# Two more FFN chunks as seven block products, two filler slots a cycle, and convolution taps issued one slot after their copy

## The chip, the cores and the metric

The kernel runs on one core of one Trainium2 chip. The metric is the device time of one launch in microseconds; lower is better. An engine is called by its short name: PE (TensorE, matmuls; PEld are its weight loads), DVE (VectorE), ACT (ScalarE), POOL (GpSimd) and SP (SyncE, which issues most DMAs).

## What is computed

A trunk of two layers over x of 512 tokens by 1024 features, all in float32. Layer 0 mixes tokens by dilated window attention, layer 1 by a gated linear recurrence (RG-LRU). Behind each mixer stands a gated convolution FFN, which is the part that matters here:

```python
def causal_dwconv(x, w, b):
    K = w.shape[0]
    S = x.shape[1]
    xp = jnp.pad(x, ((0, 0), (K - 1, 0), (0, 0)))
    out = b
    for k in range(K):
        out = out + xp[:, k:k + S] * w[k]
    return out

def conv_ffn(x, w_up, conv_w, conv_b, w_down):
    u = causal_dwconv(x @ w_up, conv_w, conv_b)
    g, v = u[..., :D_FF], u[..., D_FF:]
    return (jax.nn.gelu(g, approximate=True) * v) @ w_down
```

D_FF is 3072, the convolution has 3 taps, and each sublayer sits between two RMS norms and is added to x.

## The kernel before

**Precision.** Every float32 product is done as three float32r products: each operand is split into a high part (ACT rounds it, line 150) and a low part (DVE subtracts, line 151), and PE multiplies high by high, high by low and low by high. One *split* is thus one ACT instruction and one DVE instruction behind it. The split parts of weights live in 16 pairs of buffers (`whi`, `wlo`); `pump` splits the next piece in a fixed list after each tile or slot (in the seven stage one piece a slot), as far as buffers allow.

**The FFN.** The 3072 features of each half of `u` (the gate half g and the value half v) are worked in 12 *chunks* of 256. A half chunk is two tiles of 128 features by 512 tokens. Some chunks are made directly: a tile is 8 x 3 matmuls that are 512 wide. The chunks in `SEVEN` (3 to 10) go another way, a *chain* for each half chunk: the weights (1024 x 256) and the normed input (1024 x 512) are cut into 2 x 2 blocks, and seven block products of 12 matmuls, 256 wide, take the place of eight (Winograd's form of Strassen's method). It needs

- sums of weight blocks: two by DMA that adds into the raw weights (line 187, issued by POOL), two on DVE (lines 211 and 215, `across` and `lower`);
- sums of input blocks, made once per FFN by `token_sums` on DVE and split into the tiles `T` (four pairs; ACT casts them and DVE makes the low part);
- sums of products: ACT copies three products aside (`part`, line 1028); DVE adds one of them to the upper half when step 3 is done (line 1032, called the *join* here) and carries step 7's product over to the other half of its bank before step 4 writes the first half again (line 1037, the *carry*).

Then the convolution: ACT's *copy* `u` of the finished bank, with weight and bias (line 774), two DVE *taps* (line 776) that add the shifted bank to u, and, behind a gate half, ACT's gelu (line 789), behind a value half DVE's gate product (line 793).

**The order.** The schedule is written out by hand: each engine's instructions stand in the order in which the program emits them. In `seven` that order is a table of slots: chain n starts at slot `CYCLE * n`, and `AT` places its steps 1, 5, 2, 6, 3, 7, 4 at slots 0, 1, 2, 4, 5, 8 and 13 (13 being slot 3 of the next cycle). The slots in `FREE` (6, 7, 9) take *fillers*: quarters of the last two direct tiles, and *row products*, the first half of the down projection's columns for one block of 128 features and two of the four token tiles (6 matmuls, 512 wide), accumulated in four PSUM banks. Each block of features costs two splits, one of its row weights and one of its activation. A slot with nothing in it is not emitted. `later(n, f)` emits f after the PE work of the n+1st emitted slot from there on, ahead of that slot's pump: the join, the carry, the copy and the gelu or gate are emitted so.

```python
    AT = {1: 0, 5: 1, 2: 2, 6: 4, 3: 5, 7: 8, 4: 13}
    CYCLE, FREE = 10, (6, 7, 9)
```

Before the seven stage the FFN makes chunks 0 and 1 and, directly too, chunk 11 and half of chunk 2 (the other half of 2 is the fillers' quarters). `token_sums` starts with the first tile of chunk 1 and goes on by one step a tile. Behind the stage, `down` does the remaining row products.

Of the kernel before, what the change touches and what calls it, by code (L numbers as in the profile page):

```python
# [19 lines left out]
S = 512  # L20
# [15 lines left out]
TOE_BUFS = 2  # L36
CP_PAD = 8
WARM = 5
SEVEN = range(3, 11)
LAST, TAIL, REST = 11, 16, range(18, 22)  # L40
EARLIER = (0, 1, 2, 3, 22, 23, *range(4, 18))
AT = {1: 0, 5: 1, 2: 2, 6: 4, 3: 5, 7: 8, 4: 13}
CYCLE, FREE = 10, (6, 7, 9)
EARLY = 16
QUAD = {1: 0, 5: 2, 2: 3, 6: 4, 3: 6, 7: 8, 4: 12}
APART, ROUND = 7, 44
# [38 lines left out]
def kernel(  # L85
# [107 lines left out]
    def free_slots(n):  # L193

        end = CYCLE * n
        free = [CYCLE * c + r for c in range(n) for r in FREE][2:] + [end, end + 1]
        assert not {CYCLE * c + a for c in range(n) for a in AT.values()} & set(free)
        return free

    def stream(i0, n):  # L200

        items = []
        for c in range(n):
            i, o = i0 + c, CYCLE * c

            def left(i=i):
                add_rows(blocks(i)["w11"], plan[i][3][0][0][:, 0:4, P:256])

            def across(i=i):
                x = blocks(i)  # L210
                nc.vector.tensor_tensor(x["s1"], x["w11"], x["a22"], op=ALU.add)
# [17 lines left out]
        at = 8  # L229
# [128 lines left out]
    def side(steps, delay=1):  # L358
        sides.append([delay, steps])
# [405 lines left out]
    def ffn(layer, hT, post, pre):  # L765
        ca, cc = ffn_cols[layer]
        neg = cp.tile([P, 144], F32, tag="neg", name=nm("neg"))
        nc.vector.tensor_scalar(neg[:, 0:96], ca, -1.0, None, op0=ALU.mult)
        nc.vector.tensor_scalar(neg[:, 96:144], cc[:, 0:48], -1.0, None, op0=ALU.mult)

        def conv(ps, j, minus=False):
            u = gen(s="u")
            near, far, own = (neg, neg, neg[:, 96:144]) if minus else (ca, ca, cc)
            nc.scalar.activation(u, ps, AF.Identity, scale=own[:, j : j + 1], bias=cc[:, 48 + j : 49 + j])  # L774
            for d, wc in ((1, near[:, 48 + j : 49 + j]), (2, far[:, j : j + 1])):
                nc.vector.scalar_tensor_tensor(  # L776
                    u[:, d:], ps[:, : S - d], wc, u[:, d:], op0=ALU.mult, op1=ALU.add
                )
            return u

        gv, ready = {}, set()

        def begin(b, ps, j, minus=False):
            m = b % 2
            k = 2 * j + m
            u = conv(ps, 24 * (b // 2) + k, minus)
            if b < 2:
                gv[k] = u
                return lambda: nc.scalar.activation(u, u, AF.Gelu_apprx_tanh)
# [12 lines left out]
        def gen_load(*srcs):  # L802
            o = []

            def load():
                for src in srcs:
                    o.append(gen(s="dw"))
                    nc.sync.dma_start(o[-1].rearrange("p (k c) -> p k c", c=src.shape[-1]), src)

            return o, load  # L810

        def act(k):
            assert k in ready, k
            return gv[k]

        direct = []
        for k in EARLIER:
            w = ffn_w_down[layer][k * P : (k + 1) * P, 0:512].rearrange("(k p) c -> p k c", p=P)
            o, load = gen_load(w)
            direct.append((("rows", k), load, lambda o=o: [o[0]], 0))  # L820
            direct.append((("act", k), None, lambda k=k: [act(k)], 2))
        up["direct"] = direct
        T = []
        for j in range(SEVEN[0] - 1):
            if j:
                side(token_sums(hT, T), 0)
                tiles(j, chunk(), (0, 1))
                tiles(j, chunk(), (2, 3))
            else:
                feat_tiles(2, hT, lambda b, ps: begin(b, ps, j)(), True)  # L830
        for j in (SEVEN[0] - 1, LAST):
            tiles(j, chunk(), (0, 1))
        tiles(LAST, chunk(), (2, 3))
        prep, run = down(act, post, pre)
        return run(seven(hT, T, begin, chunk(), lambda: prep(2)))

    def down(act, post, pre):

# [75 lines left out]
    def token_sums(hT, T, first=False):  # L914

        if not first:
            assert len(sides) == 1
# [122 lines left out]

        return lambda n: lambda: step(n)

    def seven(hT, T, begin, last, prep):

        right = rights(hT, T)
        i0, acc, ends_at = state["next"], {}, CYCLE * 2 * len(SEVEN)

        def finish(b, ps, j, minus=False):
            later(1, begin(b, ps, j, minus))

        def ends(j, half):
            return lambda ps: finish(2 * half, ps, j), lambda ps: finish(2 * half + 1, ps, j, True)
# [7 lines left out]
            if pair[-1] == 3:  # L1060
                done(2)

        fill = []
        for m in range(2):
            fill += quarters(last, m, hT, lambda ps, m=m: finish(2 + m, ps, SEVEN[0] - 1))
        fill += [lambda k=k, p=p: rows(k, p) for k in EARLIER for p in ((0, 1), (2, 3))]
        steps = {}
        n = 0
        for j in SEVEN:
# [544 lines left out]
    for layer in range(2):  # L1614
        if layer:
# [8 lines left out]
        chunks = [(j, half) for j in range(SEVEN[0]) for half in range(2)]  # L1624
        chunks[-1:] = [(LAST, 0), (LAST, 1), chunks[-1]]
        for j, half in chunks + [(j, half) for j in SEVEN for half in range(2)]:
# [89 lines left out]
```

## Time and profile before

| what | value |
|---|---|
| median of 3 runs (lowest, highest) | 1420.18 us (1419.66, 1420.43) |
| the profiled execution: its own time | 1419.78 us |
| its span in the profile | 1418.0 us |
| granted PE clock, mean | 0.999 |
| seven stage of the first FFN, first step to last | 568 to 794 us |
| seven stage of the second FFN | 1108 to 1335 us |
| DMA, mean over the span | 141 GB/s |

A profile row of a timeline gives the start in us, the duration in us, the engine, the line, the operation and the tiles (out<-in), and in brackets the engine's idle time before it and what ended that idle time. A row of a group gives the count, then busy us and mean ns of one, then the idle time of the engine just before such instructions. Durations contain the time that an instruction overlaps the next one; starts of neighbours give the time for which it holds its engine. A row of the chain of waits gives start, length and what work ended last there.

### The profile page before, as it was taken

The page shows a single profiled execution, that of the slowest core. Times are in us where ns is not written, and L with a number is a line of the kernel's source. Part 1 is how long each engine was busy: PE and PEld are TensorE (multiplying, and loading weights), DVE is VectorE, ACT ScalarE, POOL GpSimd, SP SyncE. Part 2 cuts the span into 40 slices and gives each one's busy share as a digit, 9 for nine tenths or more (in the row PEclk, how much of TensorE's full clock was granted, in tenths as well). Part 3 has the DMA queues.
Part 4 walks back from the last instruction along what each step waited for, and adds up shares of the span by engine and source line. Part 5 has one row for each costly group of instructions (what it writes and reads, how often), then busy time and mean ns, then how long its engine had stood idle before and what let it go on. Part 6 is the DMA issues. An engine that isn't in the chain of part 4 may idle for free.

```text
span 1418.0 us, 23252 instructions
## 1 busy us (share of the span) xinstructions
PE 1407.8 (99%) x8597; PEld 1262.2 (89%) x8597; DVE 1108.9 (78%) x2173; ACT 782.5 (55%) x1622; POOL 215.3 (15%) x336
## 2 busy tenths in 40 slices
PE   9999999999999999999999999999999999999998
PEld 7888999999998898999999889888898999999886
DVE  6676898887866988988888758769788988888843
ACT  7343565353636554666656545589454655666641
POOL 0341332131310100212120001000101211111000
PEclk9999999999999999999999999999999999999999
DMA  7653464655665453756563632432444566665411
GB/s 227 180 144 111 120 181 152 173 160 164 172 189 187 153 178 82 171 120 164 120 156 84 221 119 90 134 119 73 136 149 112 120 139 144 154 130 127 167 57 59
DMA packets 167657, 199.79 MB, mean 141 GB/s; under 512 B 10432, under 2 KB 136856, under 8 KB 167288
## 3 DMA queue, kind: packets, MB, share of 16 engines
q1 hardware_dynamic: 123064, 153.34, 33.8%
q0 software_dynamic: 43632, 43.92, 16.6%
q8 instruction: 67, 1.10, 0.3%
q10 hardware_dynamic: 848, 1.05, 0.2%
q14 instruction: 46, 0.38, 0.1%
HBM read 179.31 MB, written 18.96 MB: 140 GB/s over the span
## 4 chain that ended last, share of the span: by engine, by line
PE 77%; DVE 4%; ACT 4%; issue 1%; DVEq 0%; ACTq 0%
PE ps L1019 31%; PE acc L413 25%; PE ps L413 13%; PE v L1212 6%; DVE wlo L151 1%; DVE xb L1517 1%; PE O L1424 1%; PE S L1358 1%; ACT whi L150 1%; ACT sig L1538 1%; PE tr L503 1%; ACT sig L1557 0%; ACT a L1555 0%; ACT xhi L150 0%; ACT th L1556 0%
## 5 line engine op out<-in xcount | busy, mean ns | idle before, releaser
L151 DVE TENSOR_TENSOR wlo<-raw,whi 128x512 fp32r<-128x512 f32 x608 | 397.2, 685 | 103.6 <-ACT whi L150 101.0
L150 ACT ACTIVATE whi<-raw 128x512 fp32r<-128x512 f32 x608 | 358.8, 625 | 156.4 <-PE ps L1019 53.1
L413 PE MATMUL ps<-hT,whi 128*128 128x512 f32 (+1 forms) x1216 | 327.5, 357 | 0.0
L1019 PE MATMUL ps<-T,whi 128*128 128x256 f32 x1536 | 280.4, 282 | 1.4 <-DVE ps L1037 1.4
L1019 PEld LDWEIGHTS ps<-T,whi 128*128 128x128 f32 x1536 | 238.9, 189 | 5.6 <-DVE ps L1037 2.0
L413 PEld LDWEIGHTS ps<-hT,whi 128*128 128x128 f32 x1216 | 214.8, 189 | 31.4
L413 PE MATMUL ps<-hT,wlo 128*128 128x512 f32 (+1 forms) x608 | 216.2, 356 | 0.0
L1019 PE MATMUL ps<-T,wlo 128*128 128x256 f32 x768 | 215.0, 280 | 0.0
L1019 PE MATMUL ps<-hT,whi 128*128 128x256 f32 x1152 | 212.8, 283 | 0.0
L1019 PEld LDWEIGHTS ps<-hT,whi 128*128 128x128 f32 x1152 | 181.5, 191 | 3.2
L1019 PE MATMUL ps<-hT,wlo 128*128 128x256 f32 x576 | 162.9, 283 | 0.0
L187 POOL DMA_DIRECT2D raw<-in_ffn_w_up_dram x64 | 82.5, 1320 | 433.8 <-DVE wlo L151 356.2
L1019 PEld LDWEIGHTS ps<-T,wlo 128*128 128x128 f32 x768 | 146.0, 190 | 0.0
L413 PE MATMUL acc<-whi,ahi 128*128 128x512 f32 x352 | 137.5, 391 | 0.0
L413 PE MATMUL acc<-whi,alo 128*128 128x512 f32 x352 | 137.2, 390 | 0.2
L413 PE MATMUL acc<-wlo,ahi 128*128 128x512 f32 x352 | 137.0, 389 | 0.0
L776 DVE SCALAR_TENSOR_TENSOR u<-ps,cols,u 128x511 f32<-128x511 f32 (+1 forms) x128 | 95.8, 749 | 45.7 <-ACT u L774 43.3
L413 PEld LDWEIGHTS ps<-hT,wlo 128*128 128x128 f32 x608 | 114.9, 189 | 16.5
L774 ACT ACTIVATE u<-ps,cols 128x512 f32<-128x512 f32 x64 | 49.8, 778 | 113.6 <-DVE ps L1032 69.9
L1019 PEld LDWEIGHTS ps<-hT,wlo 128*128 128x128 f32 x576 | 110.2, 191 | 0.0
L1212 PE MATMUL v<-whi,hT 128*128 128x512 f32 x320 | 106.5, 396 | 0.0
L1028 ACT ACTIVATE part<-ps 128x256 f32<-128x256 f32 x144 | 54.3, 377 | 70.8 <-PE ps L1019 67.3
(206 smaller groups left out, 2125.4 us busy)
## 6 DMA issues: line engine op xcount, KB each, us to landing
raw<-in_ffn_w_up_dram SPq DMA_DIRECT2D x48, 1024.0 KB
raw<-in_attn_w_qkv_dram SPq DMA_DIRECT2D x67, 512.0 KB
raw<-in_ffn_w_up_dram POOLq DMA_DIRECT2D x64, 256.0 KB, 4.7
raw<-in_ffn_w_down_dram SPq DMA_DIRECT2D x14, 1024.0 KB
dw<-in_ffn_w_down_dram SPq DMA_DIRECT2D x40, 256.0 KB
raw<-in_lru_w_in_dram SPq DMA_DIRECT2D x8, 1024.0 KB
turned<-T POOLq DMA_DIRECT2D x26, 256.0 KB, 2.6
ft<-turned POOLq DMA_DIRECT2D x104, 64.0 KB, 4.6
```

Of the source, the lines that this page charges most:

```text
L150: nc.scalar.activation(hi, raw, AF.Copy)
L151: nc.vector.tensor_tensor(lo, raw, hi.bitcast(F32), op=ALU.subtract)
L187: nc.gpsimd.dma_start(to, src, accum_op=ALU.add)
L413: mm(dst, l[a], r[b], start=start and n == 0, stop=stop and n == 2)
L503: nc.tensor.transpose(ps[:, k * P : (k + 1) * P], xs[i][:, k * P : (k + 1) * P], ident)
L774: nc.scalar.activation(u, ps, AF.Identity, scale=own[:, j : j + 1], bias=cc[:, 48 + j : 49 + j])
L776: nc.vector.scalar_tensor_tensor(u[:, d:], ps[:, : S - d], wc, u[:, d:], op0=ALU.mult, op1=ALU.add)
L1019: mm(dst, W[wa][0][:, k, :], right[n](ha, k), start=n in (1, 5) and k == q == 0, stop=k == 3 and q == 2, skip_group_check=True,)
L1028: later(1, lambda: nc.scalar.activation(to, dst, AF.Copy))
L1212: mm(bank, hT[a][:, k, t * P : (t + 1) * P], W[b][k % 2][:, 0, :], start=(k, a, b) == (0, 0, 0), stop=(k, a, b) == (KD - 1, 1, 0),)
L1358: mm(ps[:, c], q[hh][:, c], k[hh][:, c], start=True, stop=True)
L1424: mm(po[:, c], vtile(v, r, 2 * gi + hh), pts[gi][:, r], start=gi == 0, stop=gi == 1)
```

## The change

Chunks 2 and 11 join `SEVEN`, which is now 2 to 11: four more chains per FFN, 20 instead of 16. Only chunks 0 and 1 are direct, and the quarters are gone. The fillers are the 20 row blocks alone, 0 to 19 in order, in slots 6 and 7 of each cycle (slot 7 alone in the first two cycles, and two slots at the end). Slot 9 holds nothing any more, so that a cycle has nine slots. `token_sums` starts earlier, at the fifth of the eight half tiles of chunk 0. In the seven stage the two taps are emitted one slot after their copy.

```diff
-SEVEN = range(3, 11)
-LAST, TAIL, REST = 11, 16, range(18, 22)
-EARLIER = (0, 1, 2, 3, 22, 23, *range(4, 18))
+SEVEN = range(2, 12)
+TAIL, REST = 16, range(20, 24)
-CYCLE, FREE = 10, (6, 7, 9)
+CYCLE = 10
...
-        free = [CYCLE * c + r for c in range(n) for r in FREE][2:] + [end, end + 1]
+        free = [CYCLE * c + r for c in range(n) for r in ((6, 7) if c > 1 else (7,))] + [end, end + 1]
...
             nc.scalar.activation(u, ps, AF.Identity, scale=own[:, j : j + 1], bias=cc[:, 48 + j : 49 + j])
-            for d, wc in ((1, near[:, 48 + j : 49 + j]), (2, far[:, j : j + 1])):
-                nc.vector.scalar_tensor_tensor(
-                    u[:, d:], ps[:, : S - d], wc, u[:, d:], op0=ALU.mult, op1=ALU.add
-                )
-            return u
+
+            def taps():
+                for d, wc in ((1, near[:, 48 + j : 49 + j]), (2, far[:, j : j + 1])):
+                    nc.vector.scalar_tensor_tensor(
+                        u[:, d:], ps[:, : S - d], wc, u[:, d:], op0=ALU.mult, op1=ALU.add
+                    )
+
+            return u, taps
...
-            u = conv(ps, 24 * (b // 2) + k, minus)
+            u, taps = conv(ps, 24 * (b // 2) + k, minus)
+            if apart:
+                later(0, taps)
+            else:
+                taps()
...
         T = []
-        for j in range(SEVEN[0] - 1):
+        side(token_sums(hT, T), 5)
+        for j in range(SEVEN[0]):
             if j:
-                side(token_sums(hT, T), 0)
                 tiles(j, chunk(), (0, 1))
                 tiles(j, chunk(), (2, 3))
             else:
                 feat_tiles(2, hT, lambda b, ps: begin(b, ps, j)(), True)
-        for j in (SEVEN[0] - 1, LAST):
-            tiles(j, chunk(), (0, 1))
-        tiles(LAST, chunk(), (2, 3))
...
         def finish(b, ps, j, minus=False):
-            later(1, begin(b, ps, j, minus))
+            later(1, begin(b, ps, j, minus, True))
...
-        fill = []
-        for m in range(2):
-            fill += quarters(last, m, hT, lambda ps, m=m: finish(2 + m, ps, SEVEN[0] - 1))
-        fill += [lambda k=k, p=p: rows(k, p) for k in EARLIER for p in ((0, 1), (2, 3))]
+        fill = [lambda k=k, p=p: rows(k, p) for k in range(REST[0]) for p in ((0, 1), (2, 3))]
```

The loading order of the chunks and the pieces of the row weights follow the new numbers.

The first place is DVE's order in a cycle in the middle of the first FFN's seven stage, from the sum `lower` to the carry. Before (L1032 is the join, L776 the taps, L793 the gate, L1037 the carry; `raw`, `dw` and the `u` of an earlier chunk are split):

```order
L215 TENSOR_TENSOR raw_7720<-raw_7720 128x4x128
L151 TENSOR_TENSOR wlo_8149<-raw_7720,whi_8148 128x512
L1032 TENSOR_TENSOR ps_8062<-ps_8062,part_8050 128x512
L776 SCALAR_TENSOR_TENSOR u_8160<-ps_8062,cols_1202,u_8160 128x511
L776 SCALAR_TENSOR_TENSOR u_8160<-ps_8062,cols_1202,u_8160 128x510
L151 TENSOR_TENSOR wlo_8165<-dw_7907,whi_8164 128x512
L151 TENSOR_TENSOR wlo_8175<-u_7102,whi_8174 128x512
L793 TENSOR_TENSOR u_7991<-u_7991,u_8160 128x512
L151 TENSOR_TENSOR wlo_8192<-raw_7720,whi_8191 128x512
L1037 TENSOR_TENSOR ps_8037<-ps_8037,part_8051 128x256
```

And now (the same instructions are L214, L150, L1035, L777 and L799 there), from the split ahead of the lower pair of taps to one short of the carry:

```order
L150 TENSOR_TENSOR wlo_8113<-dw_7861,whi_8112 128x512
L777 SCALAR_TENSOR_TENSOR u_8110<-ps_7863,neg_5805,u_8110 128x511
L777 SCALAR_TENSOR_TENSOR u_8110<-ps_7863,neg_5805,u_8110 128x510
L150 TENSOR_TENSOR wlo_8132<-u_7474,whi_8131 128x512
L214 TENSOR_TENSOR raw_7744<-raw_7744 128x4x128
L1035 TENSOR_TENSOR ps_8042<-ps_8042,part_8035 128x512
L150 TENSOR_TENSOR wlo_8147<-raw_7744,whi_8146 128x512
L777 SCALAR_TENSOR_TENSOR u_8144<-ps_8042,cols_1202,u_8144 128x511
L777 SCALAR_TENSOR_TENSOR u_8144<-ps_8042,cols_1202,u_8144 128x510
L150 TENSOR_TENSOR wlo_8159<-raw_7744,whi_8158 128x512
L799 TENSOR_TENSOR u_7985<-u_7985,u_8144 128x512
L150 TENSOR_TENSOR wlo_8176<-raw_7903,whi_8175 128x512
```

A split now stands between the join and its taps, and two splits stand between these taps and the carry where three stood.

The second place is ACT's order there. Before, and then now (L774 and L773 are the copy, L150 and L149 the high parts of splits):

```order
L150 ACTIVATE whi_8148<-raw_7720 128x512
L789 ACTIVATE u_8126<-u_8126 128x512
L774 ACTIVATE u_8160<-ps_8062,cols_1206 128x512
L150 ACTIVATE whi_8164<-dw_7907 128x512
L150 ACTIVATE whi_8174<-u_7102 128x512
```

```order
L149 ACTIVATE whi_8077<-raw_7903 128x512
L149 ACTIVATE whi_8094<-raw_7744 128x512
L773 ACTIVATE u_8110<-ps_7863,cols_1206,neg_5805 128x512
L149 ACTIVATE whi_8112<-dw_7861 128x512
L1031 ACTIVATE part_8035<-ps_8022 128x256
L149 ACTIVATE whi_8131<-u_7474 128x512
L795 ACTIVATE u_8110<-u_8110 128x512
L773 ACTIVATE u_8144<-ps_8042,cols_1206 128x512
L149 ACTIVATE whi_8146<-raw_7744 128x512
```

ACT's order has not moved: the high half of the next split stands right behind the copy. It is `whi_8146` whose low half DVE now has ahead of the taps.

The third place is ACT's order where the first FFN's seven stage begins, from the last casts of T to the copies of the first chain's products (`part`). Before:

```order
L150 ACTIVATE T_6148<-B_6448 128x512
L150 ACTIVATE T_6149<-B_6450 128x512
L150 ACTIVATE whi_6494<-raw_6252 128x512
L150 ACTIVATE whi_6499<-raw_6160 128x512
L774 ACTIVATE u_6530<-ps_6505,cols_1206 128x512
L150 ACTIVATE whi_6534<-raw_6160 128x512
L150 ACTIVATE whi_6538<-raw_6160 128x512
L150 ACTIVATE whi_6558<-raw_6252 128x512
L1028 ACTIVATE part_6556<-ps_6543 128x256
```

And now:

```order
L149 ACTIVATE T_5997<-B_6290 128x512
L149 ACTIVATE T_5998<-B_6292 128x512
L149 ACTIVATE whi_6326<-raw_5649 128x512
L1031 ACTIVATE part_6320<-ps_6307 128x256
L149 ACTIVATE whi_6348<-raw_6009 128x512
L1031 ACTIVATE part_6321<-ps_6334 128x256
```

The casts, which stood a whole tile ahead of the first copy, now stand one split ahead of it.

More of the change, by code (lines that the diff above doesn't have):

```diff
@@ L228, in stream @@
         direct = up["direct"]
-        at = 8
+        at = 0
         for key, loads, cuts, length in direct:
@@ L774, in conv, with begin @@
             nc.scalar.activation(u, ps, AF.Identity, scale=own[:, j : j + 1], bias=cc[:, 48 + j : 49 + j])
-            for d, wc in ((1, near[:, 48 + j : 49 + j]), (2, far[:, j : j + 1])):
-                nc.vector.scalar_tensor_tensor(
-                    u[:, d:], ps[:, : S - d], wc, u[:, d:], op0=ALU.mult, op1=ALU.add
-                )
-            return u
+            def taps():
[4 more added lines that the diff above has]
+            return u, taps
         gv, ready = {}, set()
-        def begin(b, ps, j, minus=False):
+        def begin(b, ps, j, minus=False, apart=False):
             m = b % 2
             k = 2 * j + m
-            u = conv(ps, 24 * (b // 2) + k, minus)
+            u, taps = conv(ps, 24 * (b // 2) + k, minus)
[3 more added lines that the diff above has]
+                taps()
             if b < 2:
@@ L816, in ffn @@
         direct = []
-        for k in EARLIER:
+        for k in range(REST[0]):
             w = ffn_w_down[layer][k * P : (k + 1) * P, 0:512].rearrange("(k p) c -> p k c", p=P)
@@ L830, in ffn @@
                 feat_tiles(2, hT, lambda b, ps: begin(b, ps, j)(), True)
-        for j in (SEVEN[0] - 1, LAST):
-            tiles(j, chunk(), (0, 1))
-        tiles(LAST, chunk(), (2, 3))
         prep, run = down(act, post, pre)
-        return run(seven(hT, T, begin, chunk(), lambda: prep(2)))
+        return run(seven(hT, T, begin, lambda: prep(2)))
     def down(act, post, pre):
@@ L916, in token_sums @@
         if not first:
-            assert len(sides) == 1
+            assert len(sides) == 1, len(sides)
             d = dp.tile([P, 4, D], F32, name=nm("x_kept"))
@@ L1041, in chain, with seven @@
         return lambda n: lambda: step(n)
-    def seven(hT, T, begin, last, prep):
+    def seven(hT, T, begin, prep):
         right = rights(hT, T)
@@ L1623 @@
                 w_rows(lru_w_out[0], c * 256)
-        chunks = [(j, half) for j in range(SEVEN[0]) for half in range(2)]
-        chunks[-1:] = [(LAST, 0), (LAST, 1), chunks[-1]]
-        for j, half in chunks + [(j, half) for j in SEVEN for half in range(2)]:
+        for j, half in [(j, half) for j in range(12) for half in range(2)]:
             w_cols(ffn_w_up[layer], half * D_FF + j * 256, kind="seven" if j in SEVEN else "feat")
```

## The prediction

> **What bounds the kernel now.** I read the page's first part, then who makes PE wait, then the chain of waits, then the stretches of single cycles.
>
> ```profile
> PE 1407.8 (99%) x8597; PEld 1262.2 (89%) x8597; DVE 1108.9 (78%) x2173; ACT 782.5 (55%) x1622; POOL 215.3 (15%) x336
> PE ps L1019 <- DVE ps L1037: 1.4, 2, 0.7
> ```
>
> The second row is from the list of PE's waits: in the whole span PE waits twice, 0.7 us each, for a block-product carry (L1037), once in the seven stage of the second FFN. Nothing else holds it in either FFN, so PE's work sets the time there. The chain of waits gives that work piece by piece (start, us, what):
>
> ```profile
> 455.32 27.22 PE acc L413 x120
> 568.04 8.56 PE ps L1019 x72
> 691.05 8.58 PE ps L1019 x72
> 699.63 2.75 PE acc L413 x12
> 702.38 1.42 PE ps L1019 x12
> 703.80 1.39 PE acc L413 x6
> ```
>
> The last four rows are one cycle: seven block products (84 matmuls, 10.00 us, 1.43 a step) and three filler slots (4.14), 14.14 in all. A 512-wide matmul is 27.22/120 = 0.2268 us; a direct half chunk has 48 of them, 10.89 us, a block-product half chunk 10.00. How much room do the other engines have in a cycle? The stretches (length, then PE, PEld, DVE, ACT, POOL):
>
> ```profile
> 662.78:676.92 14.14, 14.14 (x105) 13.39 (x104) 11.53 (x19) 9.37 (x18) 2.58 (x2) 1.00 0.66 150
> 676.92:691.05 14.13, 14.13 (x104) 13.38 (x104) 12.33 (x21) 7.96 (x16) 2.57 (x2) 1.00 0.59 131
> sum 98.93, PE 98.93 PEld 93.68 DVE 83.89 ACT 59.89 POOL 18.02; mean PE 14.13 PEld 13.38 DVE 11.98 ACT 8.56 POOL 2.57
> ```
>
> Over seven cycles DVE works 11.98 of 14.13 us. The groups of that window say what fills the other 2.15 (busy, mean ns | idle before):
>
> ```profile
> L776 DVE SCALAR_TENSOR_TENSOR u<-ps,cols,u 128x511 f32<-128x511 f32 x7 | 5.3, 750 | 6.1 <-ACT u L774 6.1
> L151 DVE TENSOR_TENSOR wlo<-raw,whi 128x512 fp32r<-128x512 f32 x50 | 32.7, 686 | 7.4 <-ACT whi L150 6.9
> L151 DVE TENSOR_TENSOR wlo<-dw,whi 128x512 fp32r<-128x512 f32 x10 | 6.8, 685 | 1.1 <-ACT whi L150 1.1
> ```
>
> The taps wait 6.1/7 = 0.87 us a cycle for the copy; the remaining 1.2 is waiting for split halves, much of it with ACT itself waiting for PE (0.89 before 710.44 below, where ACT's preceding copy waited for PE). So DVE has roughly 1.2 us of true room in a cycle.
>
> **The change part by part.** *PE.* Four half chunks per FFN, eight in all, go from 10.89 to 10.00: 8 x 0.89 = 7.1 us saved. Row products stay 20 features x 4 token tiles. The new cycle is 10.00 + 2.75 = 12.75 us.
>
> *DVE and ACT in the new cycle.* What must now fit into 12.75 comes from these rows, DVE first, then ACT:
>
> ```profile
> 701.28 0.69 DVE L1032 TENSOR_TENSOR ps<-ps,part 128x512 f32<-128x512 f32 x1
> 702.88 1.53 DVE L776 SCALAR_TENSOR_TENSOR u<-ps,cols,u 128x511 f32<-128x511 f32 x2 [0.91 <-ACT u L774]
> 704.33 0.68 DVE L151 TENSOR_TENSOR wlo<-dw,whi 128x512 fp32r<-128x512 f32 x1
> 704.93 0.69 DVE L151 TENSOR_TENSOR wlo<-u,whi 128x512 fp32r<-128x512 f32 x1
> 706.73 0.42 DVE L1037 TENSOR_TENSOR ps<-ps,part 128x256 f32<-128x256 f32 x1
> 707.07 1.89 DVE L151 TENSOR_TENSOR wlo<-raw,whi 128x512 fp32r<-128x512 f32 x3
> 710.44 1.29 DVE L151 TENSOR_TENSOR wlo<-raw,whi 128x512 fp32r<-128x512 f32 x2 [0.89 <-ACT whi L150]
> 715.50 0.69 DVE L1032 TENSOR_TENSOR ps<-ps,part 128x512 f32<-128x512 f32 x1
> ```
>
> ```profile
> 709.79 1.14 ACT L150 ACTIVATE whi<-raw 128x512 fp32r<-128x512 f32 x2
> 716.23 0.78 ACT L774 ACTIVATE u<-ps,cols 128x512 f32<-128x512 f32 x1 [2.96 <-DVE ps L1032]
> 716.91 1.14 ACT L150 ACTIVATE whi<-raw 128x512 fp32r<-128x512 f32 x2
> 574.67 0.63 ACT L150 ACTIVATE whi<-raw 128x512 fp32r<-128x512 f32 x1 [0.50 <-DVE raw L211]
> 579.71 0.63 ACT L789 ACTIVATE u<-u 128x512 f32<-128x512 f32 x1 [0.62 <-DVE u L776]
> ```
>
> A 512-wide DVE instruction holds the engine 0.60 us (704.33 to 704.93), a pair of taps 1.45 (702.88 to 704.33), the carry 0.34 (706.73 to 707.07). The cycle issues 9 splits, two block sums (L211, L215), a join (L1032), a carry, two pairs of taps and on average one gate: 13 x 0.60 + 0.34 + 2.90 = 11.0. That is one split less than now: the filler slot dropped.
>
> The waits grow, and this decides. The move of the taps does not take away the wait between join and copy. It puts a split between join and taps, and that split's high half stands behind the copy in ACT's own order. From join to copy 0.73 (715.50 to 716.23), copy 0.68 (to 716.91), high half to low half 0.65 (709.79 to 710.44): the split starts 2.06 after the join, of which the join takes 0.60. DVE stands idle 1.46 a cycle, where now the taps wait 0.9 and the split is ready when they end. The same for the lower pair: now the taps run while ACT goes on from copy to split; then a split stands ahead of them. The sum L211 releases ACT's high half after 0.72 (573.95 to 574.67), then 0.52 for it, 0.68 copy, 0.65: 2.57, in which DVE has L211 and two splits, 1.8: idle 0.77. In gate cycles the gelu starts 0.1 after the taps (579.71), and the second split behind waits 0.1 + 0.53 + 0.65 less 0.60 = 0.7, in half of the cycles 0.35. (Rows for the two starts:)
>
> ```profile
> 573.95 0.68 DVE L211 TENSOR_TENSOR raw<-raw 128x512 f32<-128x512 f32 x1
> 578.09 1.53 DVE L776 SCALAR_TENSOR_TENSOR u<-ps,cols,u 128x511 f32<-128x511 f32 x2 [0.85 <-ACT u L774]
> ```
>
> Sum 11.0 + 1.46 + 0.77 + 0.35 = 13.6 us for DVE's loop against 12.75 for PE's. The bounds: with only the join's wait real, 12.5; with busy time from the stretches instead of intervals (11.98 - 0.60 = 11.38) and all waits, 14.0. I take 13.65, between walk and upper end, since each wait rests on a fixed order of both queues.
>
> *Where PE meets it.* Step 4 of a chain overwrites what the carry reads. Today step 7 ends at 703.80, the carry runs from 706.73 to 707.15, and step 4 comes after a filler and three steps, at 703.80 + 1.39 + 3 x 1.43 = 709.48: 2.3 us to spare. The filler that is dropped there takes 1.39 of that, and a loop 0.9 too long uses up the rest in one cycle. From then on PE waits 0.9 at step 4 in every cycle. Weight pieces lie many steps ahead and do not help.
>
> *The start.* The corrections T had ten direct tiles of cover; now they begin at the fifth half tile of chunk 0 and have four half tiles and four tiles. The block products start six tiles (24 x 0.2268 = 5.44 each) earlier, at 568.04 - 6 x 5.44 = 535.4. From the second tile's taps on,
>
> ```profile
> 511.13 1.52 DVE L776 SCALAR_TENSOR_TENSOR u<-ps,cols,u 128x511 f32<-128x511 f32 x2
> 511.00:543.00 32.00, 32.00 (x153) 26.91 (x153) 28.72 (x45) 16.77 (x29) 1.32 (x1) 1.00 0.47 140
> ```
>
> DVE, which today does 28.7 us in those 32, must get through 7 pairs of taps (10.2) and 36 other instructions (21.6) before the last T's second half can be cast: 511.1 + 31.8 = 542.9. In ACT's order the copy of step 1's product stands behind those two casts and one split: it ends about 545. PE wants it for step 6 at 535.4 + 3 x 1.43 = 539.7. Stall 5.5. Below it at least 3.5 (if the taps overlap better), above it 7.5 (if DVE also waits for casts). The first carry is one more microsecond late by the same count, as the join's wait comes ahead of it: 6.5 together.
>
> *Sum per FFN.* -3.55 saved, +6.5 start, 17 middle cycles x 0.9 = 15.3, first cycle (one filler only) 1.3, last cycle (double splits of the next weights, shorter for PE) 3: +22.5. Twice: +45. The profiled execution took 1419.78, so 1464.8; the median of the three runs is 0.4 above it: 1465. At the ends: loop 12.5 leaves start alone, 2 x (6.5 - 3.55) = +6, 1426; loop 14.0 gives 2 x (6.5 + 17 x 1.25 + 5 - 3.55) = +58, 1478.
>
> **Rivals.** (1) *PE stays the bound.* By occupancy DVE would have 11.38 of 12.75 us, 89%; were its waits to shrink under load and the start to fit, the full 7.1 is gained: 1413. For it: PE never waits in steady cycles today. Against it: the waits come from the order of two queues, each of which the rows show running in the program's order, not from a lack of rate. The Trainium skill (Perfetto Trace Analysis, Identifying the Most-Contended Engine) names the engine of highest occupancy as the one to optimize, which after the change would still be PE; by that rule this rival holds. Today's cycles agree with it (PE 14.13 of 14.13), but they are no test of it, since no engine there waits long enough to hold PE.
>
> (2) *The start alone.* Loop at or under 12.75 because ACT runs ahead further than I allow; the stall at step 6 remains: 1426, slower. It decides from the point where the corrections' 31.8 us exceed the cover left.
>
> (3) *Transfers.* 1 MB of weights, two 256 KB sums and one 256 KB row block in 12.75 us is 140 GB/s, between the 131 and 150 of today's cycles; no loss by itself, and a longer cycle eases it.
>
> **How the numbers follow.** Forecast 0.72; start alone 0.12; PE bound 0.09; slower still by transfers or waits that I miss 0.07. A measurement of this kernel tells about 0.2% from no change. Faster 0.09, same 0.04 (a start that costs just what PE saves), slower 0.87. Range 1425 to 1482; the forecast's own is 1446 to 1480.
>
> **What would show it.** Right: PE's waits list the carry some 18 times per FFN, about 0.9 each, and one of about 5 us for ACT's part copy at the start; cycles of 13.4 to 14 us in the chain; DVE idle about 1.4 ahead of the split that follows each join; no wait of taps for copies. Wrong: cycles of 12.75 with PE unbroken (rival 1), or one gap at the start and then 12.75 (rival 2).

## The result, and the profile after

The changed kernel took 1468.53 us (median of 4 runs, 1467.82 to 1469.21), the kernel before 1419.92 beside it (1419.52 to 1420.43): a ratio of 1.0342, with a 95% interval of 1.0324 to 1.036. It is 48.6 us slower; 45 were predicted (1465 us).

The page's first part and the whole list of PE's waits, of the changed kernel (what waits, for what: us in total, times, longest):

```profile
PE 1415.0 (97%) x8885; PEld 1276.8 (87%) x8885; DVE 1141.5 (78%) x2229; ACT 791.4 (54%) x1670; POOL 234.8 (16%) x352
```

```profile
PE ps L1022 <- DVE ps L1040: 30.5, 39, 1.8
PE ps L1022 <- ACT part L1031: 11.0, 2, 5.5
```

Before, PE waited 1.4 us for the carry in the whole span. Now it waits 39 times, 0.78 us each, for the carry (L1040 is the old L1037; 38 of the waits are in the two FFNs), and once per FFN 5.5 us for a copied product (L1031). All engines are busy for shares that look harmless: DVE's 78% is what it was.

Two neighbouring cycles of the first FFN, each from the start of one step 5 to the start of the next, with one step 4 in it (length, then busy time of PE, PEld, DVE, ACT, POOL, granted clock, DMA share, GB/s):

```profile
661.77:675.81 14.04, 12.99 (x99) 12.29 (x97) 11.34 (x19) 8.90 (x19) 2.55 (x2) 1.00 0.58 130
675.81:689.09 13.28, 12.99 (x99) 12.30 (x97) 11.25 (x19) 6.56 (x13) 2.57 (x2) 1.00 0.58 132
sum 27.32, PE 25.98 PEld 24.59 DVE 22.59 ACT 15.47 POOL 5.11; mean PE 12.99 PEld 12.29 DVE 11.29 ACT 7.73 POOL 2.56
```

Cycles take 14.04 and 13.28 us in turn, on average 13.66; PE's own work in one is 12.75. The wait at step 4, PE's timeline at two successive ones:

```profile
665.83 0.38 PE L1022 MATMUL ps<-T,whi 128*128 128x256 f32 x1 [1.05 <-DVE ps L1040]
...
679.11 0.50 PE L1022 MATMUL ps<-T,whi 128*128 128x256 f32 x2 [0.29 <-DVE ps L1040]
```

Why 13.66 is read from DVE's timeline in the same stretch, from one join (L1035) to the next (13.88 us here; the loop before it, from the join at 659.27 to that at 672.72, took 13.45), with the gelu's wait of a later gate cycle as the last row, and from ACT's behind the first join:

```profile
672.72 0.69 DVE L1035 TENSOR_TENSOR ps<-ps,part 128x512 f32<-128x512 f32 x1
674.77 0.69 DVE L150 TENSOR_TENSOR wlo<-raw,whi 128x512 fp32r<-128x512 f32 x1 [1.36 <-ACT whi L149]
675.38 1.53 DVE L777 SCALAR_TENSOR_TENSOR u<-ps,cols,u 128x511 f32<-128x511 f32 x2
...
682.74 0.69 DVE L150 TENSOR_TENSOR wlo<-dw,whi 128x512 fp32r<-128x512 f32 x1 [0.49 <-ACT whi L149]
683.35 1.53 DVE L777 SCALAR_TENSOR_TENSOR u<-ps,neg,u 128x511 f32<-128x511 f32 x2
...
686.60 0.69 DVE L1035 TENSOR_TENSOR ps<-ps,part 128x512 f32<-128x512 f32 x1
...
774.04 0.69 DVE L150 TENSOR_TENSOR wlo<-raw,whi 128x512 fp32r<-128x512 f32 x1 [0.68 <-ACT whi L149]
```

```profile
673.45 0.78 ACT L773 ACTIVATE u<-ps,cols 128x512 f32<-128x512 f32 x1 [1.12 <-DVE ps L1035]
674.12 2.19 ACT L149 ACTIVATE whi<-raw 128x512 fp32r<-128x512 f32 x4
```

The taps wait for nothing any more. The split between join and taps waits 1.36 us instead: ACT had stood idle for 1.12 us with that split's high half second in its queue, because the copy in front of it waited for the join.

At the start of the stage, PE's timeline on both sides of its first long wait, and the granted clock there (the same columns as above):

```profile
539.58 0.40 PE L1022 MATMUL ps<-hT,whi 128*128 128x256 f32 x2
539.82 0.28 PE L1022 MATMUL ps<-hT,wlo 128*128 128x256 f32 x1
545.59 0.80 PE L1022 MATMUL ps<-T,whi 128*128 128x256 f32 x2 [5.49 <-ACT part L1031]
546.19 0.41 PE L1022 MATMUL ps<-T,wlo 128*128 128x256 f32 x1
546.40 0.63 PE L1022 MATMUL ps<-T,whi 128*128 128x256 f32 x2
```

```profile
545.00:548.00 3.00, 2.41 (x11) 2.41 (x12) 3.00 (x6) 1.33 (x4) 0.00 (x0) 0.50 0.00 0
548.00:552.00 4.00, 4.00 (x21) 3.78 (x21) 3.81 (x7) 2.05 (x4) 1.27 (x1) 0.71 0.80 246
```

Behind the wait PE runs at half the granted clock: a pair of matmuls takes 0.63 us instead of 0.40. In the chain of waits the two steps behind it are one piece:

```profile
543.52 1.23 ACT T L149 x2
545.59 5.22 PE ps L1022 x24
550.82 1.39 PE acc L412 x6
```

Two steps are 2 x 1.43 = 2.86 us. Here the filler behind them begins 5.06 us after their start (545.59 to 550.65; the 5.22 of the row goes on to the end of the last matmul, which overlaps the filler): 2.2 more. In the second FFN it begins after 4.40 us (1110.29 to 1114.69), 1.5 more. This explains why PE is listed as *busier* than before (1415.0 against 1407.8) with 7.1 us less to do. The span's 48.0 us are 40.8 of idle time (1466.0 - 1415.0 against 1418.0 - 1407.8; 40.1 of it the waits listed above), -7.1 of work, and 14.3 that are listed as busy time. Of these the slow matmuls behind the two stalls are 3.7. Most of the rest stands at the carry waits: the two cycles above are 27.32 - 25.50 = 1.82 longer than PE's work, their two listed waits are 1.05 and 0.29; the missing 0.48 is 0.24 a wait, about 9 for 39. It is listed as busy because the last matmul ahead of a wait counts for 0.28 us, where the next one would start after 0.12, and the pair behind the wait holds PE for 0.34 us instead of 0.24 (665.83 to 666.17). Some 1.5 more are a slow stretch at the end of the first FFN's stage (last section).

### The profile page after: what moved, and what is told of

Same layout as the page of the kernel before. It is cut to its first block, busy times and chain, and to the rows that moved or that the text cites. A ratio compares the mean times of both kernels' runs of the same rounds, so it can differ in the third digit from the quotient of the medians.

```text
span 1466.0 us, 23772 instructions
## 1 busy us (share of the span) xinstructions
PE 1415.0 (97%) x8885; PEld 1276.8 (87%) x8885; DVE 1141.5 (78%) x2229; ACT 791.4 (54%) x1670; POOL 234.8 (16%) x352
## 3 DMA queue, kind: packets, MB, share of 16 engines
q10 hardware_dynamic: 848, 1.05, 0.2%
## 4 chain that ended last, share of the span: by engine, by line
PE 49%; DVE 30%; ACT 15%; issue 3%; DMA 1%; POOL 0%; DVEq 0%; ACTq 0%; POOLq 0%
PE acc L412 16%; PE ps L1022 11%; DVE wlo L150 10%; PE ps L412 9%; DVE u L777 8%; PE v L1212 7%; ACT whi L149 7%; ACT u L773 4%; DVE u L799 2%; DVE raw L210 2%; DVE ps L1035 2%; DVE raw L214 2%; PE v L1150 1%; DVE xb L1517 1%; PE O L1424 1%
## 5 line engine op out<-in xcount | busy, mean ns | idle before, releaser
L150 DVE TENSOR_TENSOR wlo<-raw,whi 128x512 fp32r<-128x512 f32 x632 | 417.9, 687 | 144.0 <-ACT whi L149 139.8
L149 ACT ACTIVATE whi<-raw 128x512 fp32r<-128x512 f32 x632 | 371.9, 624 | 175.6 <-PE ps L1022 47.2
L1022 PE MATMUL ps<-T,whi 128*128 128x256 f32 x1792 | 333.8, 286 | 41.5 <-DVE ps L1040 30.5
L1022 PEld LDWEIGHTS ps<-T,whi 128*128 128x128 f32 x1792 | 280.6, 191 | 54.7 <-DVE ps L1040 39.1
L1022 PE MATMUL ps<-T,wlo 128*128 128x256 f32 x896 | 252.5, 282 | 0.0
L1022 PE MATMUL ps<-hT,whi 128*128 128x256 f32 x1344 | 249.2, 284 | 0.0
L412 PE MATMUL ps<-hT,whi 128*128 128x512 f32 (+1 forms) x960 | 248.4, 348 | 0.0
L1022 PE MATMUL ps<-hT,wlo 128*128 128x256 f32 x672 | 190.2, 283 | 0.0
L1022 PEld LDWEIGHTS ps<-T,wlo 128*128 128x128 f32 x896 | 171.6, 192 | 0.0
L412 PE MATMUL ps<-hT,wlo 128*128 128x512 f32 (+1 forms) x480 | 166.5, 347 | 0.0
L773 ACT ACTIVATE u<-ps,cols 128x512 f32<-128x512 f32 x56 | 43.4, 774 | 96.9 <-DVE ps L1035 92.9
L1031 ACT ACTIVATE part<-ps 128x256 f32<-128x256 f32 x168 | 62.6, 372 | 53.2 <-PE ps L1022 53.0
L777 DVE SCALAR_TENSOR_TENSOR u<-ps,cols,u 128x511 f32<-128x511 f32 x112 | 83.6, 747 | 6.7 <-ACT u L773 4.7
```

What stands on the lines that cost most here:

```text
L149: nc.scalar.activation(hi, raw, AF.Copy)
L150: nc.vector.tensor_tensor(lo, raw, hi.bitcast(F32), op=ALU.subtract)
L412: mm(dst, l[a], r[b], start=start and n == 0, stop=stop and n == 2)
L777: nc.vector.scalar_tensor_tensor(u[:, d:], ps[:, : S - d], wc, u[:, d:], op0=ALU.mult, op1=ALU.add)
L1022: mm(dst, W[wa][0][:, k, :], right[n](ha, k), start=n in (1, 5) and k == q == 0, stop=k == 3 and q == 2, skip_group_check=True,)
L1031: later(1, lambda: nc.scalar.activation(to, dst, AF.Copy))
```

## The experiments

Ratios are to the kernel before, timed on the same chip in the same session. Line numbers move a little from kernel to kernel; the tiles (`ps`, `u`, `wlo`, `part`) name the instruction.

**taps_at_once** undoes the taps' delay and keeps all else.

```diff
         def finish(b, ps, j, minus=False):
-            later(1, begin(b, ps, j, minus, True))
+            later(1, begin(b, ps, j, minus))
```

> Undoes one part: each pair of taps stands directly behind its copy again, all else as changed. Theory A (DVE's loop is lengthened by the split that stands between join and taps, whose high half waits behind the copy): the 1.36 us gap behind each join becomes a wait of about 0.9 us of the taps for the copy, the split behind it is ready, and the cycle falls from 13.66 to between 12.75 and 13.2; with 17 cycles in two FFNs that gives back 16 to 31 us: 1437 to 1453 us. Rival B (the cycle is long because two fillers leave DVE too little PE time, whatever the order of the taps): 1463 to 1472 us.

Measured: 1431.55 us, ratio 1.0086 (1.0071 to 1.0101). This is about 37 us back, and 5 us below theory A's range; rival B is out. The bound of 13.2 in that expectation was too careful: the loop fell below PE's 12.75 and the carry waits went from 39 to 3 (one of them, as before, outside the FFNs):

```profile
PE ps L1022 <- DVE ps L1040: 3.6, 3, 1.4
```

**before_taps_late** puts the delay alone into the kernel before (the same edit of `conv`, `begin` and `finish` as in the change, with 16 chains and three fillers).

> Does one part alone: the kernel before, with its three fillers and 16 chains, but with the taps one slot behind their copy. Theory A: DVE's loop becomes one split longer than after the change, 13.66 + 0.60 = about 14.2 us, against PE's 14.14, so PE waits little or nothing: 1419 to 1425 us. Rival B as before gives no change either, 1420 us; a rival C, that late taps cost PE their wait directly in every cycle, gives 14 cycles x 2 x 0.9 = 25 us more, 1445 us.

Measured: 1424.15 us, ratio 1.0037 (1.0025 to 1.005). The delay alone costs 4.9 us, within A's range; C is out. Two neighbouring cycles between joins:

```profile
689.65:703.92 14.27, 14.27 (x105) 13.48 (x104) 11.34 (x19) 9.03 (x17) 2.97 (x3) 1.00 0.64 148
703.92:717.88 13.96, 13.96 (x103) 13.25 (x102) 12.36 (x21) 8.01 (x16) 2.16 (x2) 1.00 0.61 134
```

PE works without a break there, 14.12 us a cycle, and DVE keeps that pace: its own loop, about 14.2 by theory A's count, is about as long and does not show by itself. The third filler's 1.39 us of PE time had paid for the longer loop. Of the 4.9 us, 2.4 are carry waits (one of 1.57 us in each FFN); the rest is not traced to a place. So the delay alone costs little, and taps_at_once shows the dropped filler alone to cost nothing in the cycles; a loop of 13.66 meets a cycle of 12.75 only when both are done.

**copy_behind_split** keeps the delay, and moves ACT's copy behind the split of its slot. DVE's instructions are the same, in the same order.

```diff
         tick(length)
+        while behind:
+            behind.pop(0)()
...
-            nc.scalar.activation(u, ps, AF.Identity, scale=own[:, j : j + 1], bias=cc[:, 48 + j : 49 + j])
+
+            def copy():
+                nc.scalar.activation(u, ps, AF.Identity, scale=own[:, j : j + 1], bias=cc[:, 48 + j : 49 + j])
+
+            behind.append(copy) if apart else copy()
```

> As changed, but in the seven stage ACT's copy is issued behind the slot's split, so that the split's high half stands ahead of the copy in ACT's order; DVE's order is the same instruction for instruction. Theory A: the split behind the join finds its high half ready, the taps wait about 0.3 us for the copy, and DVE's cycle falls from 13.66 to about 11.9 us, below PE's 12.75: cycles of 12.75, carry waits gone, only the two stalls at the start left (5.5 us each and some us of slower matmuls behind them): 1426 to 1440 us. Rival B (DVE's work, not the order of ACT's queue, is too much for the cycle): 1460 us or more.

Measured: 1431.55 us, ratio 1.0087 (1.0072 to 1.0102). Theory A holds; B falls, since DVE does the same work in the same order. DVE's timeline behind a join, and two cycles:

```profile
677.00 0.69 DVE L1041 TENSOR_TENSOR ps<-ps,part 128x512 f32<-128x512 f32 x1
677.60 0.68 DVE L150 TENSOR_TENSOR wlo<-raw,whi 128x512 fp32r<-128x512 f32 x1
678.54 1.53 DVE L783 SCALAR_TENSOR_TENSOR u<-ps,cols,u 128x511 f32<-128x511 f32 x2 [0.26 <-ACT u L777]
```

```profile
667.90:680.70 12.80, 12.80 (x99) 12.31 (x99) 11.18 (x19) 6.78 (x13) 2.57 (x2) 1.00 0.66 145
680.70:693.40 12.70, 12.70 (x98) 12.21 (x97) 11.22 (x19) 8.95 (x18) 2.56 (x2) 1.00 0.63 143
```

The 1.36 us became 0 and 0.26, the cycle 12.75. What remains is the start, and a little at the end, as the list of PE's waits of this kernel says:

```profile
PE ps L1028 <- ACT part L1037: 11.0, 2, 5.5
PE ps L1028 <- DVE ps L1046: 3.6, 3, 1.4
```

**carry_at_once** issues the FFN's carries one slot earlier in the changed kernel.

```diff
-                later(1, lambda: nc.vector.tensor_tensor(y[1][:, 256:512], dst, t[1][:, 0:256], op=ALU.add))
+                later(int(not up), lambda: nc.vector.tensor_tensor(y[1][:, 256:512], dst, t[1][:, 0:256], op=ALU.add))
```

> As changed, but in the FFNs' seven stage the carry is issued one slot earlier (it moves ahead of one split, in gate cycles also ahead of the gelu's wait, 0.6 to 1.9 us on DVE). Theory A: the loop of DVE is the bound and the carry only the place where PE meets it; the waits move to another step or stay at 0.7 us a cycle, and the time falls by no more than once 2 us per FFN: 1464 to 1469 us. Rival D (the carry's place is the cause; step 4 waits for it because it stands too late): the 39 waits of 0.8 us shrink by 0.6 us or more each, 1435 to 1447 us.

Measured: 1465.53 us, ratio 1.0325 (1.0309 to 1.034). Theory A: 3.0 us, not 21 or more. The carry is only the place where PE meets the loop: in the cycles the waits shrink from 1.05 and 0.29 in turn to 0.82 and 0.28, and the one at each stage's last carry grows from 1.8 to 3.0. There still are 37 such waits:

```profile
PE ps L1022 <- DVE ps L1040: 26.3, 37, 3.0
```

Now the start. **dummies_at_start** adds PE work to copy_behind_split, which nothing reads:

```diff
         for m in range(max(steps) + 1):
+            if m == AT[6]:
+                spare = psum("warm")
+                for _ in range(24):
+                    mm(spare, hT[0][:, 0, :P], hT[0][:, 0, :], start=True, stop=True)
```

> As copy_behind_split, and ahead of the first chain's step 6 PE makes 24 matmuls of 512 columns into a spare bank that nothing reads (24 x 0.2268 = 5.44 us, as long as the stall there). Theory A2 (behind the stall of 5.5 us PE runs for some 4.7 us at half the granted clock, 0.43 us instead of 0.24 for a pair of 256-wide matmuls, because it had stood still): with PE kept busy the 12 matmuls of step 6 take 1.4 us instead of 2.7, step 3 1.4 instead of 2.3, and each FFN ends 2.2 us earlier: 1426 to 1428.5 us from 1431.55. Rival E (the matmuls behind the stall are slow because their operands arrive slowly): they stay slow, 1430.5 to 1433 us.

Measured: 1426.93 us, ratio 1.0051 (1.0038 to 1.0065), 4.6 below copy_behind_split. The stretch behind the stall (columns as for the cycles above), in copy_behind_split and then here:

```profile
546.00:549.00 3.00, 3.00 (x16) 3.00 (x16) 2.91 (x6) 1.00 (x3) 0.00 (x0) 0.50 0.11 15
```

```profile
545.00:548.00 3.00, 2.97 (x20) 2.44 (x19) 3.00 (x6) 2.01 (x5) 0.00 (x0) 1.00 0.00 0
```

The clock stays at 1.00 when PE does not stand still. So the stall costs 5.5 us plus 2.3 of half-speed matmuls behind it, in each FFN; E is out.

**gate2_direct** and **chunk2_direct** put direct work back ahead of the stage, on top of copy_behind_split: the gate half of chunk 2 in the first, all of chunk 2 in the second, with the corrections beginning later there.

```diff
-SEVEN = range(2, 12)
+CHAINS = [(2, 1)] + [(j, half) for j in range(3, 12) for half in range(2)]
...
-        free = [CYCLE * c + r for c in range(n) for r in ((6, 7) if c > 1 else (7,))] + [end, end + 1]
+        free = [CYCLE * c + r for c in range(n) for r in (6, 7)] + [end, end + 1]
...
+        tiles(2, chunk(), (0, 1))
```

```diff
-SEVEN = range(2, 12)
+SEVEN = range(3, 12)
...
-        free = [CYCLE * c + r for c in range(n) for r in ((6, 7) if c > 1 else (7,))] + [end, end + 1]
+        free = [CYCLE * c + r for c in range(n) for r in ((6, 7) if c > 1 else (6, 7, 9))] + [end, end + 1]
...
-        side(token_sums(hT, T), 5)
         for j in range(SEVEN[0]):
             if j:
+                if j == 1:
+                    side(token_sums(hT, T), 0)
```

> As copy_behind_split, but the gate half of chunk 2 is made directly before the stage: 19 chains instead of 20 per FFN, two more direct tiles (10.9 us of PE work, 5.9 of DVE's) between the input corrections and the first chain, and two fillers in every cycle. Theory A (the start stalls because DVE is 5.5 us behind with the corrections): 5.0 us more of cover and two more fillers in the first two cycles take the stalls away, with the slow matmuls behind them; PE's own work grows by 2 x 0.89: 1419.3 - 7.1 + 1.8 = 1414 and at most 5 of remaining waits, 1414 to 1419 us. Rival F (the first product copy is late by its own place in ACT's queue, whatever the cover): the stalls stay, 1429 to 1434 us.

> As copy_behind_split, but all of chunk 2 is made directly before the stage, with the corrections beginning at chunk 1 as in the kernel before: 18 chains per FFN, three fillers in the first two cycles, two in the others. Theory A: no stall at the start; PE's work grows by 4 x 0.89 = 3.6 over copy_behind_split's: 1419.3 - 7.1 + 3.6 = 1415.8 and at most 3 of waits, 1415.5 to 1419 us. Rival F: as for gate2_direct, stalls of 5 us twice, 1427 to 1433 us.

Measured: 1422.34 us, ratio 1.002 (1.0011 to 1.0029), and 1424.01, ratio 1.0033 (1.0021 to 1.0045). Both missed their ranges by 3 and 5 us. With 10.9 us more of direct work between corrections and stage the stall shrank from 5.5 to 1.8, so cover is most of what it lacked:

```profile
PE ps L1029 <- ACT part L1038: 3.6, 2, 1.8
```

A wait of 1.37 us at each stage's last carry, which copy_behind_split has too, is the other part of the miss. In chunk2_direct the stall is 2.0 although DVE is no longer behind: its last direct taps had to wait for their copy. DVE's timeline there, and ACT's:

```profile
558.29 1.53 DVE L783 SCALAR_TENSOR_TENSOR u<-ps,cols,u 128x511 f32<-128x511 f32 x2 [0.89 <-ACT u L777]
559.74 1.28 DVE L945 TENSOR_TENSOR B<-hT,hT 128x512 f32<-128x512 f32 x2
560.94 1.29 DVE L951 SCALAR_TENSOR_TENSOR B<-B,B 128x512 f32<-128x512 f32 x2
```

```profile
561.65 1.23 ACT L149 ACTIVATE T<-B 128x512 fp32r<-128x512 f32 x2 [2.36 <-DVE B L951]
562.79 0.61 ACT L149 ACTIVATE whi<-raw 128x512 fp32r<-128x512 f32 x1
563.31 0.36 ACT L1038 ACTIVATE part<-ps 128x256 f32<-128x256 f32 x1
```

The product copy stands behind the casts of the last T, and these wait for the sums B that DVE makes behind the last direct tile's taps. A and F are each half right.

**gate2_direct_late_taps** is gate2_direct with ACT's copy ahead of the split again.

> As gate2_direct, but ACT's copy stands ahead of the slot's split, as in the change. Theory A: start and loop are two separate losses. The loop stays at 13.66 us a cycle; the stalls at the start go (2 x (5.65 + 2.2) = 15.7), while PE's work grows by 1.8 and meets the slow loop a cycle or so later: 1468.5 - 15.7 + 1.8 = 1454.6, with one less cycle of 0.9 lost in each FFN 1452 to 1457 us. Rival G (one backlog of DVE, so that the time won at the start is lost again at the carries, whose waits rise above 0.8 us until PE has fallen back): 1462 to 1470 us.

Measured: 1456.26 us, ratio 1.0258 (1.0244 to 1.0272). Start and loop add up, as A said, and G is out: the carry waits are 0.75 us on average. The stalls did not go, as A had it; they are 1.8 us as in gate2_direct, so that A's sum of 1454.6 leaves out some 4 us there.

```profile
PE ps L1029 <- DVE ps L1047: 27.8, 37, 1.8
```

**gate2_sums_later** moves the last T's sums and splits into the first cycle.

```diff
-        yield 1 + first
+        yield 2 if first else 7
         b21 = whole(4, 0)
...
-        yield 1 + first
+        yield 2 if first else 3
         parted(3, b21)
```

> As gate2_direct, but the last input sum and its split pair T (8 DVE instructions, 4.8 us), which only step 4 reads, are issued in the middle of the first cycle instead of ahead of the stage. Theory A (what is left at the start, 1.78 us of waiting for the first product copy in each FFN, is DVE's work in front of the last direct taps, behind whose gelu the copy stands): the two waits go, and the first carry keeps its margin of about 1.9 us by 0.1: 1422.3 - 3.6 = 1418.7, 1417.5 to 1420 us. Rival H (the backlog only moves to the first carry): 1421 to 1423.5 us with new carry waits of over 1 us.

Measured: 1419.42 us, ratio 1.0001 (0.9992 to 1.0009). The time lies in A's range, but the trace is H's: the wait for the product copy is gone, and in its place PE waits 1.46 us at the first carry. A forgot that DVE issues the moved instructions in front of that carry.

```profile
563.93 0.47 PE L1029 MATMUL ps<-T,whi 128*128 128x256 f32 x2 [1.46 <-DVE ps L1047]
```

The gain of 2.9 us is more than these waits' difference, 2 x (1.78 - 1.46) = 0.6, while the two profiled executions, both at a mean granted clock of 0.999, differ by 0.7 (1420.57 and 1419.86); the last section says where the rest may be.

**gate2_both_ends** was meant to issue the last carry ahead of four splits.

```diff
+            f = chain(right, *ends(j, half), last=n == len(CHAINS) - 1)
...
-                later(1, lambda: nc.vector.tensor_tensor(y[1][:, 256:512], dst, t[1][:, 0:256], op=ALU.add))
+                later(0 if last else 1, lambda: nc.vector.tensor_tensor(y[1][:, 256:512], dst, t[1][:, 0:256], op=ALU.add))
```

> As gate2_sums_later, and the carry of the last chain alone is issued one slot earlier, ahead of two weight splits, two activation splits and a gate (3 us) that now stand in front of it. Theory A (the last wait of 1.37 us per FFN is that order): another 2 x 1.37 us, 1418.7 - 2.7 = 1416, 1414.5 to 1417.5 us, under the kernel before (1419.3). Rival H: 1418 us or more, because DVE is then late for the activations of the rows that follow.

Measured: 1419.57 us, ratio 1.0003 (0.9994 to 1.0012). This run decides nothing. In the last cycle no split is issued between those two slots, and every engine's order came out as in gate2_sums_later.

**carry_soon_at_ends** makes the three moves that the trace of that kernel asks for.

```diff
-        yield 2 if first else 7
+        yield 2
         b21 = whole(4, 0)
-        if first:
-            yield 2
+        yield 2 if first else 5
...
-            f = chain(right, *ends(j, half), last=n == len(CHAINS) - 1)
+            f = chain(right, *ends(j, half), soon=n in (0, len(CHAINS) - 1))
...
-            if m == ends_at - 2:
-                prep()
             if m in steps:
                 slot(steps[m])
+            if m == ends_at:
+                prep()
```

> As gate2_both_ends, with three moves that its trace asks for: the first chain's carry too is issued one slot earlier (0.6 us), the two sums of the last input correction (1.2 us) go into a gap of 1.4 us that DVE has ahead of the stage's first instructions, and the splits of the first two activations (1.2 us) stand behind the last carry instead of ahead of it. Theory A (each wait left is DVE's order in front of a carry): the wait of 1.46 at the first carry falls below 0.3, that of 1.36 at the last below 0.4, twice each: 1419.5 - 2 x (1.2 + 1.0) = 1415.1, 1414 to 1417 us. Rival I (the waits are DVE's amount of work and come back at the next step that waits): 1418 us or more.

Measured: 1414.65 us (1414.2 to 1414.9, 6 runs), ratio 0.9967 (0.9955 to 0.9979): 4.6 us under the kernel before. Theory A holds: the wait at the first carry is gone and the one at the last is 0.16 us in each FFN (the 0.9 below stands outside the FFNs). The three moves were made together, so no run says what each is worth. PE's busy time and what is left of its carry waits:

```profile
PE 1401.9 (99%) x8813; PEld 1267.4 (90%) x8813; DVE 1128.8 (80%) x2215; ACT 790.1 (56%) x1658; POOL 230.3 (16%) x348
```

```profile
PE ps L1028 <- DVE ps L1046: 1.2, 3, 0.9
```

## Why the prediction was right, and where it was off

**PE's saving** (7.1 us, cycles of 12.75): right. With the loop out of the way the two cycles of copy_behind_split average 12.75, and its total adds up: -7.1, 11.0 of stalls, 4.6 of slow matmuls, 2.7 at the two last carries and 0.24 for each of these four waits are 12.2 us over the kernel before; 12.3 were measured.

**DVE's loop** (13.65 us): right, and shown, not only summed. Measured 13.66; the wait behind the join 1.36 (forecast 1.46), that ahead of the lower taps 0.49 plus 0.2 inside the pair ahead of it (0.77), the gelu's 0.68 in each gate cycle (0.7). That the sum agrees to 0.01 is luck: the waits came out 0.2 shorter than forecast and the instructions 0.2 longer. Its cause, a high half behind a copy in ACT's order, was tested by moving nothing but the stage's copies: about 37 of the 48.6 us came back.

**Where PE meets it** (step 4, 0.9 us a cycle): right. 0.67 of it is listed as waits (1.05 and 0.29 in turn), 0.24 hides in busy time. The waits came 19 times per FFN (some 18 forecast). Moving the carry gave 3.0 us, so the place was only the place.

**The start** (a stall of 5.5 us and 1.0 more at the first carry): the stall was 5.49 and 5.50 us, and for the forecast reason: in the first FFN DVE worked with no pause longer than 0.1 us from 511.55 to 544.09, 32.5 us against the 31.8 counted. The 1.0 did not come as a carry wait. In its place came a term that the sum did not have: PE's half clock behind the stall, 2.2 us in the first FFN and 1.5 in the second. It also gave DVE the time to be ready for the first carry: in the first FFN that carry ended at 556.74 and step 4 began at 557.74, so that a step 4 2.2 us earlier would have waited some 1.2 (worked out from these rows, not tried). And the stall had two causes. The prediction counted DVE's backlog and the copy's place in ACT's order as one time; the runs part them: cover took the stall from 5.5 to 1.8 us, and the rest was order, ACT's copy behind instructions that wait for DVE.

**The first cycle** (1.3 us) came to nothing, it seems for the same reason: PE's first carry wait comes one carry later, 0.54 and 1.19 us. **The last** (3 us) was mis-sized: its two waits are 1.57 and 1.80 with 0.24 each behind them, 3.9, and in the first FFN a slow stretch behind the second of some 1.5.

**Sum.** -3.55 + 6.5 + 15.3 + 1.3 + 3 = 22.5 per FFN was forecast, 24.3 measured. The rows give 5.5 for the stall, 1.9 for the clock, 15.6 for the middle cycles, 4.6 for the last and -3.55: 24.1. So the total came this close partly by luck: the clock and the last cycle, 3.5 us too low together, stand against the first carry and the first cycle, 2.3 that did not come.

**Rival 1** (PE stays the bound, 1413 us) was the right picture of the same work in a better order: with nearly all of the FFNs' waits taken away, and one half chunk fewer as block products, it is 1414.65. The Trainium skill (Perfetto Trace Analysis, Identifying the Most-Contended Engine) would optimize the engine of highest occupancy. In the changed kernel PE has 97% and DVE 78%, and still DVE's and ACT's order set the cycle; the occupancies of the stretches, 11.29 of 13.66 for DVE, do not tell it, the waits do. **Rival 2** (the start alone, 1426) gave the size of what copy_behind_split leaves, 1431.55, too low by the clock and the last carry's waits. **Rival 3** (transfers): in no run did PE, DVE or ACT wait for a transfer in the stage; only POOL did, which issues the adding DMAs.

## What to carry to other kernels

When work is moved away from a wait, ask who issues the work that takes its place: here a split was put into the gap of one engine, but its first half stood behind the very instruction that was waited for on another engine. In a loop over two in-order queues the sum of one queue's busy time is no bound; walk the loop through both queues, waits included, and compare that with the loop of the engine that should be the bound. An issue order that lets the other queue run ahead can be worth more than the work saved: the copies moved by one place gave back some 37 us in a change that saves 7 of PE's work.

## What the runs showed of the hardware that was not expected

**A stall costs twice.** Behind 5.49 us without a matmul the granted clock was 0.50 for 3.2 to 5.4 us in the four stalls of the changed kernel and copy_behind_split, and 24 matmuls that nothing reads, put into the gap, removed that, 4.6 us for two stalls. The Trainium skill (TensorE: Matmul & The Clock Gate, Part 1: The HAM clock gate) says that the clock falls to half after an idle window of about 3.4 us; this stall agrees with it, and the next point does not.

**Shorter waits can cost it too, and not always.** In one execution of the changed kernel, two waits of the same length at the ends of the two stages:

```profile
816.22 0.52 PE L1022 MATMUL ps<-T,whi 128*128 128x256 f32 x2 [1.80 <-DVE ps L1040]
816.56 0.39 PE L1022 MATMUL ps<-T,wlo 128*128 128x256 f32 x1
816.75 0.63 PE L1022 MATMUL ps<-T,whi 128*128 128x256 f32 x2
...
1380.93 0.50 PE L1022 MATMUL ps<-T,whi 128*128 128x256 f32 x2 [1.79 <-DVE ps L1040]
1381.27 0.28 PE L1022 MATMUL ps<-T,wlo 128*128 128x256 f32 x1
1381.39 0.40 PE L1022 MATMUL ps<-T,whi 128*128 128x256 f32 x2
```

The first is followed by pairs of 0.63 us, half speed, for about 3 us, the second by pairs of 0.40. Waits of 3.04 and 3.03 us in carry_at_once have a granted clock of 0.50 behind them, both waits of 2.01 us in chunk2_direct 1.00. So a fixed length from which a wait costs the clock is not what these traces show. gate2_direct and chunk2_direct, whose profiled executions have two waits of 1.78 and of 2.01 at full clock behind them, varied more than the other experiments: 11 runs of the first from 1420.57 us, at a mean granted clock of 0.999, to 1423.63, with the three slowest at 0.996 and 0.997, and 6 of the second from 1422.69 (0.999) to 1426.01 (0.997). gate2_sums_later, with 1.46 in their place, stayed between 1419.06 and 1419.86 at 0.998 or 0.999. That the waits of about 1.8 us drop the clock in some executions would explain both the spread and the 2.9 us between gate2_direct and gate2_sums_later; it was not tried by itself.
